# Feed-forward up projections of a hybrid encoder trunk by a seven-product block algorithm, with one arena of buffers and smaller down groups

## The chip, the cores and the metric

The kernel runs on one core of a Trainium2 chip. The metric is the device time of one execution in microseconds (us), the median of several runs. The matrix engine is PE (TensorE), its weight loads are shown apart as PEld; DVE is VectorE, ACT is ScalarE, POOL is GpSimd, SP is SyncE, whose queue issues the weight loads from device memory.

## The reference

Two batches of tokens, one of 512 and one of 256, go through a trunk of two layers with shared weights. The width is 1024, the inner width of a feed-forward network (FFN) is 2816. Cut to what matters:

```python
def rmsnorm(x, g):
    return x * rsqrt(mean(x * x, axis=-1) + 1e-6) * g

def swiglu_ffn(x, w1, w2):
    gate, up = split(x @ w1, 2, axis=-1)       # w1: 1024 x 5632
    return (silu(gate) * up) @ w2              # w2: 2816 x 1024

# a layer; mixer: layer 0 bidirectional HGRN2, layer 1 windowed attention
x = x + 0.5 * swiglu_ffn(rmsnorm(x, g0), w1a, w2a)
x = x + mixer(rmsnorm(x, g1))
x = x + 0.5 * swiglu_ffn(rmsnorm(x, g2), w1b, w2b)
# after the last layer: y = rmsnorm(x, g)
```

All data are fp32. There are four FFNs: the first, then the HGRN2 mixer, then the second and the third one behind the other, then the attention mixer, then the fourth.

## The kernel before

**Layout.** Activations lie transposed: 1024 features are eight tiles of 128 partitions (index m or k, constant `NC`), tokens are columns. The two batches are `s = 0` with 512 columns and `s = 1` with 256 (`SEQS`); the residual is `self.x[s][m]`.

**Precision.** An fp32 operand is split into a high part (rounded to fp32r) and a low part (the rest). A product of two split operands is three matmuls into one PSUM bank: high·high, high·low, low·high (`mm3`, L175–179). Operands are split by a copy on ACT and a subtraction on DVE: `split` (L181–183) for activations, and `stage_next` (L139–153) for weights, with the cast at L148 and the subtraction at L149. The subtraction is on DVE or, for the first two columns of an FFN (`early`), on POOL.

**Weights.** `plan_ffn` puts all weight tiles of an FFN in a list in the order of their use. `load_next` issues the load of the next one on SP into a raw tile (`wr`, two buffers), and `stage_next` splits it into `wh` and `wl` (`WBUFS` = 4 of each). When the last matmul that reads a tile has been issued, `done` frees it and stages the next (`ahead`). So the staging instructions stand in ACT's and DVE's order at the place where a tile came free, between the operations of the column that is being computed, and each engine works through its instructions in that order.

**FFN.** The 22 columns of the inner width (128 each; a column has a gate tile and an up tile of weights) are taken in groups, `FFN_GROUPS = (7, 7, 6, 2)`. For each column `ffn_up` (L358–378) computes, for both batches in turn, gate and up by 8 k-blocks × 3 matmuls each, then Silu on ACT (L375), the product on DVE (L376), and the split of the hidden tile. After the columns of a group `ffn_down` (L380) multiplies the hidden tiles of the group by their rows of `w2` for each of the eight output tiles, and `add_x` (L388–393) adds half of the result to the residual. In the last group, of two columns, batch 0 is finished first (up, then down), then batch 1, so that the norm of batch 0 can run beside batch 1's matmuls.

**Norm.** `after_x` squares each finished residual tile and sums the squares (`sumsq`, L249–261: POOL or DVE at L259). `norm_steps` (L281–311) is a list of steps for a batch: the statistics (`rstd`, L265–279, small matmuls at L273), and two `apply` steps of four tiles each, with the normalisation on DVE (L304), the high part on ACT (L306) and the low part on DVE and POOL in turn (L308), into the operands `self.h[s][m]`. `later` puts steps on a list and `run_later` takes the next one; the calls stand between the matmuls of the next stage, so they set where the norm stands in each engine's order. For the first FFN, `enter` in `load_x` (L203–229) makes the operands from the loaded tokens.

**Memory.** `big` tiles (12 of them) hold hidden tiles, mixer data and other large things; the normed operands have a pool of their own (`hp`).

Names in rows: ps is a PSUM bank, h a normed operand, wr a raw weight tile, wh and wl its parts, tA and tB temporaries (512 and 256 columns), big a large tile, x the residual.

Of the kernel before, what the change touches and what calls it, by code (L numbers as in the profile page):

```python
# [13 lines left out]
ALU = mybir.AluOpType  # L14
# [20 lines left out]
FFN_GROUPS = (7, 7, 6, 2)  # L35
WBUFS = 4


class Trunk:
    def __init__(self, ctx, tc, consts):  # L40
# [4 lines left out]
        self.hp = pool("hp")  # L45
# [19 lines left out]
    def tmp(self, n, dt=F32):  # L65
        tag, bufs, size = ("tA", 7, TA) if n > TB else ("tB", 4, TB)
        t = self.tp.tile([P, size], dt, tag=tag, name=self.name(tag), bufs=bufs)
        return t[:, :n]

    def big(self, shape, dt=F32):  # L70
        return self.ap.tile(shape, dt, tag="big", name=self.name("big"), bufs=12)
# [9 lines left out]
    def ht(self, s, part):  # L81
        n = (TA, TB)[s]
        return self.hp.tile([P, n], F32R, tag=f"h{s}{part}", name=self.name("h"), bufs=8)
# [27 lines left out]
    def load_tables(self):  # L111
# [3 lines left out]
        mf = self.wp.tile([P, LEVELS + 1, P], F32, tag="wr", name="mf", bufs=2)  # L115
# [10 lines left out]
    def plan(self, key, src, shape, eng, spare=False):  # L126
        self.queue.append((key, src, shape, eng, spare))

    def load_next(self):
        key, src, shape, eng, spare = self.queue.pop(0)  # L130
        raw = self.wtile("wr", F32, 2, shape)
        self.last_load = self.nc.sync.dma_start(raw, src.rearrange("(k p) c -> p k c", p=P))
        self.loaded.append((key, raw, shape, eng, spare))

    def wtile(self, tag, dt, bufs, shape):
        t = self.wp.tile([P, 1024], dt, tag=tag, name=self.name(tag), bufs=bufs)
        return t[:, : shape[0] * shape[1]].rearrange("p (a b) -> p a b", a=shape[0])

    def stage_next(self):  # L139
        if not self.loaded:  # L140
            self.load_next()
        key, raw, shape, eng, spare = self.loaded.pop(0)
        if spare:
            n = shape[0] * shape[1]
            hi, lo = (self.big([P, 1024], F32R)[:, :n].rearrange("p (a b) -> p a b", a=shape[0]) for _ in range(2))
        else:
            hi, lo = (self.wtile(tag, F32R, WBUFS, shape) for tag in ("wh", "wl"))
        self.nc.scalar.copy(hi, raw)  # L148
        eng.tensor_sub(lo, raw, hi.bitcast(F32))  # L149
        self.staged[key] = (hi, lo, spare)  # L150
        self.held += not spare
        while self.queue and len(self.loaded) < 2:
            self.load_next()
# [6 lines left out]
    def done(self, key):  # L160
        self.held -= not self.staged.pop(key)[2]
        self.ahead()

    def ahead(self):
        while (self.queue or self.loaded) and self.held < WBUFS:
            self.stage_next()
# [18 lines left out]
    def load_x(self, srcs):  # L185
# [17 lines left out]
        def enter(s):  # L203
# [19 lines left out]
            self.h[s] = []  # L223
            for m in range(NC):
                g = self.cols[:, m : m + 1]
                hi, lo = self.ht(s, "h"), self.ht(s, "l")
                order[-1] = nc.scalar.activation(hi, pt(m), AF.Copy, scale=g).ins
                nc.vector.scalar_tensor_tensor(lo, pt(m), g, hi.bitcast(F32), ALU.mult, ALU.subtract)
                self.h[s].append((hi, lo))
# [17 lines left out]
        self.later(lambda: enter(1), lambda: None, lambda: None, lambda: None, residual)  # L247
# [33 lines left out]
    def norm_steps(self, s, row):  # L281
# [14 lines left out]

        def apply(part):
# [3 lines left out]
            for m in range(4 * part, 4 * part + 4):  # L301
                g = self.cols[:, row * NC + m : row * NC + m + 1]
                t = self.tmp(n)
                nc.vector.scalar_tensor_tensor(t, self.x[s][m], g, box["pb"], ALU.mult, ALU.mult)  # L304
                hi, lo = self.h[s][m]
                nc.scalar.copy(hi, t)  # L306
                eng = nc.gpsimd if m % 2 else nc.vector
                eng.tensor_sub(lo, t, hi.bitcast(F32))  # L308

        self.h[s] = [(self.ht(s, "h"), self.ht(s, "l")) for _ in range(NC)]  # L310
        return stats, lambda: apply(0), lambda: apply(1)
# [27 lines left out]
    def plan_ffn(self, tag, w1, w2):  # L339
        early, late = self.nc.gpsimd, self.nc.vector  # L340

        def up(j, spare=False):
            for c in (j, NF + j):
                eng = early if j < 2 else late
                self.plan((tag, "up", c), w1[:, c * P : (c + 1) * P], (NC, P), eng, spare)

        j = 0
        for gi, n in enumerate(FFN_GROUPS):
            last = gi == len(FFN_GROUPS) - 1
            for i in range(n):  # L350
                up(j + i, last and i == 0)
            width = 4 * P if last else P
            for c in range(D // width):
                src = w2[j * P : (j + n) * P, c * width : (c + 1) * width]
                self.plan((tag, "down", gi, c), src, (n, width), late)
            j += n

    def ffn_up(self, tag, j, seqs, hid):  # L358
        nc = self.nc
        keys = [(tag, "up", c) for c in (j, NF + j)]  # L360
        for s in seqs:
            off, n = SEQS[s]
            pss = []
            for key in keys:
                wh, wl = self.take(key)
                ps = self.ps(n)
                for k in range(NC):
                    self.mm3(ps, (wh[:, k, :], wl[:, k, :]), self.h[s][k], k == 0, k == NC - 1)
                    if k in ((6,), (4, 6))[key == keys[1]] if s == 0 else (k == NC - 1 and key == keys[0]):
                        self.run_later()  # L370
                if s:
                    self.done(key)
                pss.append(ps)
            a, u = self.tmp(n), self.tmp(n)
            self.last_act = nc.scalar.activation(a, pss[0], AF.Silu).ins  # L375
            self.last_dve = nc.vector.tensor_mul(u, a, pss[1]).ins  # L376
            self.split(u, hid[:, 0, off : off + n], hid[:, 1, off : off + n])
            self.run_later()
# [16 lines left out]
    def ffn(self, tag, next_row):  # L395
        j = 0
        for gi, n in enumerate(FFN_GROUPS[:-1]):
            hids = [self.big([P, 2, T], F32R) for _ in range(n)]
            for i in range(n):
                self.ffn_up(tag, j + i, (0, 1), hids[i])  # L400
            j += n
            for m in range(NC):
                key = (tag, "down", gi, m)
                w = self.take(key)
                for s in range(2):
                    self.ffn_down(s, m, hids, *w)
                self.done(key)
        hids = [self.big([P, 2, T], F32R) for _ in range(FFN_GROUPS[-1])]
        for s in range(2):
            for i, hid in enumerate(hids):  # L410
                self.ffn_up(tag, j + i, (s,), hid)
            for m in range(NC):
                key = (tag, "down", gi + 1, m // 4)
                c = (m % 4) * P
                self.ffn_down(s, m, hids, *(t[:, :, c : c + P] for t in self.take(key)))
                if s and m % 4 == 3:
                    self.done(key)
                self.after_x(s, m, next_row)
                if s and m < NC - 1:
                    self.run_later()  # L420
# [356 lines left out]
    def swa(self, next_row):  # L777
# [48 lines left out]
        out = [[None] * NC, [None] * NC]  # L826
        of = {}
# [371 lines left out]
```

## Time and profile before

| | |
|---|---|
| time, median of 3 runs | 3131.28 us (3129.14 to 3134.45) |
| span of the profiled execution (its own time) | 3127.9 us |
| instructions in the span | 42175 |
| PE busy | 3071.7 us, 17765 matmuls |
| PEld busy | 2705.4 us |
| DVE busy | 1313.4 us, 2254 instructions |
| ACT busy | 931.3 us, 1677 instructions |
| POOL busy | 407.5 us, 294 instructions |
| moved by DMA | 199.18 MB, mean 64 GB/s |

The profile is that of one execution. A busy time is the sum of the times of an engine's instructions; the matmuls of PE overlap in their records (one starts before the end of the one ahead is recorded), so that the cost of a matmul in a full stream is the distance between two starts. An instruction's row names its line, the operation, output and inputs with their sizes, and, in brackets, how long its engine was idle before it and what ended that. The granted clock is the share of full speed at which PE was allowed to run.

### The profile page before, as it was taken

The page shows a single profiled execution, that of the slowest core. Times are in us where ns is not written, and L with a number is a line of the kernel's source. Part 1 is how long each engine was busy: PE and PEld are TensorE (multiplying, and loading weights), DVE is VectorE, ACT ScalarE, POOL GpSimd, SP SyncE. Part 2 cuts the span into 40 slices and gives each one's busy share as a digit, 9 for nine tenths or more (in the row PEclk, how much of TensorE's full clock was granted, in tenths as well). Part 3 has the DMA queues.
Part 4 walks back from the last instruction along what each step waited for, and adds up shares of the span by engine and source line. Part 5 has one row for each costly group of instructions (what it writes and reads, how often), then busy time and mean ns, then how long its engine had stood idle before and what let it go on. Part 6 is the DMA issues. An engine that isn't in the chain of part 4 may idle for free.

```text
span 3127.9 us, 42175 instructions
## 1 busy us (share of the span) xinstructions
PE 3071.7 (98%) x17765; PEld 2705.4 (86%) x17765; DVE 1313.4 (42%) x2254; ACT 931.3 (30%) x1677; POOL 407.5 (13%) x294
## 2 busy tenths in 40 slices
PE   8999999999999999999999999999999999999998
PEld 7888888888898888888888888888877878888887
DVE  4222223467477562322234322222459862323233
ACT  4212121433333432121223311212357752121122
POOL 1000000354443130000002000000113440000000
PEclk9999999999999999999999999999999999999999
DMA  3222222211110322222221222221222112222221
GB/s 120 65 64 65 65 61 75 80 56 41 41 41 28 108 68 66 67 64 61 68 63 52 61 65 64 61 68 54 82 72 63 41 44 64 70 61 61 68 72 57
DMA packets 324797, 199.18 MB, mean 64 GB/s; under 512 B 7208, under 2 KB 308736, under 8 KB 324608
## 3 DMA queue, kind: packets, MB, share of 16 engines
q1 hardware_dynamic: 314688, 183.07, 19.6%
q10 hardware_dynamic: 9920, 13.43, 1.3%
q8 instruction: 139, 2.28, 0.3%
q14 instruction: 50, 0.41, 0.0%
HBM read 187.03 MB, written 9.44 MB: 63 GB/s over the span
## 4 chain that ended last, share of the span: by engine, by line
PE 92%; DVE 4%; ACT 2%; issue 1%; POOL 1%; DMA 1%; POOLq 0%; DVEq 0%; SPq 0%; ACTq 0%
PE ps L178 28%; PE ps L177 28%; PE ps L179 28%; PE ps L531 3%; PE ps L626 1%; PE ps L602 1%; DMA wr<-in_ffn_w_dram 0%; PE ps L1061 0%; ACT wh L148 0%; POOL tA L259 0%; DVE h L308 0%; DVE tB L259 0%; PE ps L273 0%; ACT big L1038 0%; PE ps L1022 0%
## 5 line engine op out<-in xcount | busy, mean ns | idle before, releaser
L177 PE MATMUL ps<-h,wh 128*128 128x256 f32 (+1 forms) x3200 | 1087.6, 340 | 0.1
L178 PE MATMUL ps<-h,wh 128*128 128x256 f32 (+1 forms) x3200 | 1080.1, 338 | 3.3 <-POOL h L308 3.1
L179 PE MATMUL ps<-h,wl 128*128 128x256 f32 (+1 forms) x3200 | 1077.8, 337 | 0.0
L178 PEld LDWEIGHTS ps<-h,wh 128*128 128x128 f32 x3200 | 609.4, 190 | 67.1 <-POOL h L308 4.6
L177 PEld LDWEIGHTS ps<-h,wh 128*128 128x128 f32 x3200 | 609.6, 191 | 64.2 <-issue 1.0
L179 PEld LDWEIGHTS ps<-h,wl 128*128 128x128 f32 x3200 | 608.7, 190 | 64.0
L148 ACT CAST wh<-wr 128x1024 fp32r<-128x1024 f32 (+2 forms) x344 | 346.7, 1008 | 848.7 <-PE ps L178 686.9
L177 PE MATMUL ps<-big,wh 128*128 128x256 f32 (+1 forms) x1536 | 519.0, 340 | 6.9 <-DVE tA L304 6.1
L178 PE MATMUL ps<-big,wh 128*128 128x256 f32 (+1 forms) x1536 | 520.2, 339 | 2.8 <-DVE big L183 2.8
L179 PE MATMUL ps<-big,wl 128*128 128x256 f32 (+1 forms) x1536 | 518.5, 338 | 0.1
L149 DVE TENSOR_TENSOR wl<-wr,wh 128x1024 fp32r<-128x1024 f32 (+2 forms) x276 | 322.0, 1167 | 220.7 <-ACT wh L148 218.5
L376 DVE TENSOR_TENSOR tA<-tA,ps 128x512 f32<-128x512 f32 x88 | 60.5, 687 | 717.7 <-PE ps L179 717.7
L177 PEld LDWEIGHTS ps<-big,wh 128*128 128x128 f32 x1536 | 292.7, 191 | 40.6 <-DVE tA L304 6.7
L259 POOL TENSOR_TENSOR tA<-tA,tA 128x512 f32<-128x512 f32 x36 | 46.5, 1293 | 2138.6 <-ACT tA L257 2137.0
L178 PEld LDWEIGHTS ps<-big,wh 128*128 128x128 f32 x1536 | 294.5, 192 | 34.6 <-DVE big L183 4.4
L179 PEld LDWEIGHTS ps<-big,wl 128*128 128x128 f32 x1536 | 294.4, 192 | 31.1 <-DVE wl L149 0.3
L393 DVE SCALAR_TENSOR_TENSOR x<-ps,x 128x256 f32<-128x256 f32 (+1 forms) x256 | 141.9, 557 | 398.7 <-PE ps L179 398.4
L182 ACT CAST big<-tA 128x512 fp32r<-128x512 f32 x88 | 54.5, 619 | 476.0 <-DVE tA L376 476.0
L149 POOL TENSOR_TENSOR wl<-wr,wh 128x1024 fp32r<-128x1024 f32 x68 | 166.3, 2450 | 148.7 <-ACT wh L148 145.3
L375 ACT ACTIVATE tA<-ps 128x512 f32<-128x512 f32 x88 | 52.6, 598 | 357.4 <-PE ps L179 357.4
L177 PE MATMUL ps<-wh,h 128*128 128x512 f32 x336 | 135.0, 402 | 0.6 <-DVE stat L1025 0.6
L578 DVE TENSOR_TENSOR big<-big,big 128x384 f32<-128x384 f32 x168 | 127.8, 806 | 15.5 <-ACT big L556 13.8
(183 smaller groups left out, 2784.9 us busy)
## 6 DMA issues: line engine op xcount, KB each, us to landing
wr<-in_ffn_w_dram SPq DMA_DIRECT2D x184, 512.0 KB, 3.8
wr<-in_ffn_w_dram SPq DMA_DIRECT2D x64, 448.0 KB, 3.3
wr<-in_hg_w_in_dram SPq DMA_DIRECT2D x40, 512.0 KB, 3.7
wr<-in_ffn_w_dram SPq DMA_DIRECT2D x32, 384.0 KB, 3.1
wr<-in_hg_w_o_dram SPq DMA_DIRECT2D x12, 512.0 KB, 3.6
wr<-in_sw_w_qkv_dram SPq DMA_DIRECT2D x12, 512.0 KB, 3.5
spill<-x ACTq DMA_DIRECT2D x16, 256.0 KB, 2.0
x<-spill ACTq DMA_DIRECT2D x16, 256.0 KB, 2.8
```

The source lines that it names most:

```text
L148: self.nc.scalar.copy(hi, raw)
L149: eng.tensor_sub(lo, raw, hi.bitcast(F32))
L177: nc.tensor.matmul(out, a[0], b[0], start=first, stop=False)
L178: nc.tensor.matmul(out, a[0], b[1], start=False, stop=False)
L179: nc.tensor.matmul(out, a[1], b[0], start=False, stop=last)
L182: self.nc.scalar.copy(hi, src)
L259: (nc.vector if s or m == NC - 1 else nc.gpsimd).tensor_add(self.acc[s], self.acc[s], t)
L375: self.last_act = nc.scalar.activation(a, pss[0], AF.Silu).ins
L376: self.last_dve = nc.vector.tensor_mul(u, a, pss[1]).ins
L393: self.nc.vector.scalar_tensor_tensor(x, ps, c, x, ALU.mult, ALU.add)
L531: nc.tensor.matmul(pss[s][:, i * P : (i + 1) * P], lhs(b), rhs(b), start=True, stop=True)
L578: eng.tensor_mul(xv, xv, t[td][1 - par])
```

## The change

**Seven products.** The first group of an FFN, now two columns, is computed as before (`up_plain`), except that the 768 tokens are taken as two halves of 384 columns instead of 512 and 256. Each of the other 20 columns is computed by `up_pair`: gate and up tile are seen as a 2×2 matrix of blocks (rows: gate and up; columns: features 0–511 and 512–1023), and the activations as another (features 0–511 and 512–1023; token halves 0 and 1). The product of two such matrices is made from seven block products instead of eight, in Winograd's form: seven times 4 k-blocks × 3 matmuls of 384 columns.

- The activations' sums `t1` to `t4` are made once per FFN by `sum_steps`: 16 sums on POOL, each then split on ACT and DVE. The blocks `b00`, `b10`, `b01` and `b11` are split by `put_half`. The step list of the norm is longer by these four steps.
- The weights' sums are made on DVE in `pair_steps`, which replaces the staging of a tile by seven steps, one for each product (`p1`, `p6`, `p2`, `p7`, `p5`, `p4`, `p3`): four sums of 512 elements, and for each product a cast on ACT and a subtraction, on DVE but for `p5`, whose is on POOL.
- The products' results are joined in `up_pair`: where two products are only added, they are accumulated in one PSUM bank; the rest is one copy on ACT and five additions or subtractions on DVE, between the products. Two banks are used twice: product `p2` is added to the bank that ACT has just copied, `p4` and `p3` to banks that DVE has just read.

**Groups.** `FFN_GROUPS = (2, 4, 4, 4, 4, 4)`: down projections come after two, then after every four columns. In the last group all columns' ups come first, then the down projection of batch 0, then that of batch 1. The last group's down weights are loaded and split twice, once for each batch.

**Buffers.** `hp` is gone; `SLOTS` = 18 big tiles hold the operands, sums and hidden tiles. Staged weights share `WBUFS` = 8 tiles of one kind (high and low part of a pair's product lie in one), raw weights have `RAWBUFS` = 4, `tA` has 9 buffers. The mixers' operands (`self.h`) are in big tiles too.

The diff, cut to its core:

```diff
-FFN_GROUPS = (7, 7, 6, 2)
-WBUFS = 4
+FFN_GROUPS = (2, 4, 4, 4, 4, 4)
+H = T // 2
+WBUFS = 8
+RAWBUFS = 4
+SLOTS = 18
...
+    def pair_steps(self, key, one, two):
...
+        a11, a12, a21, a22 = flat(one, 0), flat(one, 1), flat(two, 0), flat(two, 1)
...
+        def split(name, src, eng):
+            w = self.wtile()
+            hi, lo = w[:, :512], w[:, 512:]
+            nc.scalar.copy(hi, src)
+            eng.tensor_sub(lo, src, hi.bitcast(F32))
...
+        def p6():
+            box["s3"] = self.tmp(512)
+            nc.vector.tensor_add(box["s3"], a11, a21)
+            nc.vector.tensor_add(a21, a21, a22)
+            nc.vector.tensor_add(a11, a11, a21)
+            split("p6", a11, nc.vector)
...
+    def sum_steps(self):
...
+        def go(k):
+            b11, b12, b21, b22 = (self.block(i // 2, i % 2, k) for i in range(4))
+            t = {n: self.tmp(H) for n in ("t1", "t3", "t2", "t4")}
+            nc.gpsimd.tensor_sub(t["t1"], b11, b12)
+            nc.gpsimd.tensor_sub(t["t3"], b12, b22)
+            nc.gpsimd.tensor_add(t["t2"], t["t1"], b22)
+            nc.gpsimd.tensor_sub(t["t4"], b21, t["t2"])
+            for n, src in t.items():
+                self.split(src, *self.operand(n, k))
...
+    def up_pair(self, tag, j, hid):
...
+        self.product(key, "p1", "b00", a, True, False)
+        nc.scalar.copy(v, a)
+        self.product(key, "p6", "t2", b, True, True)
+        nc.vector.tensor_sub(v, v, b)
+        self.product(key, "p2", "b10", a, False, True)
+        nc.scalar.activation(g, a, AF.Silu)
+        self.product(key, "p7", "t3", c, True, False)
+        nc.vector.tensor_sub(w, c, v)
+        self.product(key, "p5", "t1", d, True, False)
+        nc.vector.tensor_sub(w, w, d)
+        self.product(key, "p4", "t4", c, False, True)
+        nc.vector.tensor_sub(u, c, v)
+        nc.vector.tensor_mul(u, u, g)
+        self.split(u, hid[:, 0, :H], hid[:, 1, :H])
+        self.product(key, "p3", "b11", d, False, True)
+        nc.vector.tensor_add(v, v, d)
+        self.last_act = nc.scalar.activation(v, v, AF.Silu).ins
+        self.last_dve = nc.vector.tensor_mul(v, v, w).ins
+        self.split(v, hid[:, 0, H:], hid[:, 1, H:])
...
+            if gi == 0:
+                for half in range(2):
+                    for i in range(n):
+                        self.up_plain(tag, i, half, hids[i])
+                self.run_later(len(self.deferred))
+            else:
+                for i in range(n):
+                    self.up_pair(tag, j + i, hids[i])
...
+            for s in range(2):
+                for m in range(NC):
+                    down(s, m, s, True)
+                    self.after_x(s, m, next_row)
+                    if s and m < NC - 1:
+                        self.run_later(1 if next_row is not None else 2)
```

In the new code the lines of the steps named later are: cast and subtraction of a product's weights L167 and L168 (of a plain tile, L152 and L153), the weights' sums L177, L178, L179 and L183, the split of an activation L239 (ACT) and L240 (DVE), the sums on POOL L411–414, the plain columns' product of gate and up L486, the matmul of a product L494, the joining operations L510 (ACT), L512, L516, L518, L520, L521, L524 and L526 (DVE), the addition to the residual L542.

PE's order in one column of the third FFN, before: with each of its two weight tiles 24 matmuls of 512 columns, of which the first two k-blocks with the up tile are shown (wh and wl are the parts of that tile, h those of the normed operand); the same follows for 256 columns.

```order
L177 MATMUL ps_13815<-h_13193,wh_13654 128x512
L178 MATMUL ps_13815<-h_13194,wh_13654 128x512
L179 MATMUL ps_13815<-h_13193,wl_13655 128x512
L177 MATMUL ps_13815<-h_13195,wh_13654 128x512
L178 MATMUL ps_13815<-h_13196,wh_13654 128x512
L179 MATMUL ps_13815<-h_13195,wl_13655 128x512
```

After, a whole column is 14 such rows of six matmuls: seven products, each with one tile w and two big tiles of the operand (here the first pair of the third FFN).

```order
L494 MATMUL ps_14651<-big_13997,w_14456 128x384 x6
L494 MATMUL ps_14651<-big_14002,w_14456 128x384 x6
L494 MATMUL ps_14652<-big_14264,w_14463 128x384 x6
L494 MATMUL ps_14652<-big_14325,w_14463 128x384 x6
L494 MATMUL ps_14651<-big_14028,w_14491 128x384 x6
L494 MATMUL ps_14651<-big_14033,w_14491 128x384 x6
L494 MATMUL ps_14653<-big_14261,w_14494 128x384 x6
L494 MATMUL ps_14653<-big_14322,w_14494 128x384 x6
L494 MATMUL ps_14654<-big_14258,w_14566 128x384 x6
L494 MATMUL ps_14654<-big_14319,w_14566 128x384 x6
```

The bank 14651 is written by the first product and, with the second one between them, again by the third; the second product's operand 14264 is one of the sums `t2`.

DVE's order at the start of the third FFN, before: behind the normalisation of batch 1 (L304, L308) come at once the first column's product (L376), its split (L183) and the staging of weights (L149).

```order
L304 SCALAR_TENSOR_TENSOR tB_13585<-x_8573,cols,ps_13549 128x256
L308 TENSOR_TENSOR h_13488<-tB_13581,h_13487 128x256
L376 TENSOR_TENSOR tA_13593<-tA_13592,ps_13533 128x512
L183 TENSOR_TENSOR big_13491<-tA_13593,big_13491 128x512
L149 TENSOR_TENSOR wl_13624<-wr_13421,wh_13623 128x1024
L376 TENSOR_TENSOR tB_13661<-tB_13660,ps_13629 128x256
L149 TENSOR_TENSOR wl_13655<-wr_13471,wh_13654 128x1024
```

After, behind the normalisation stand 16 splits of sums (L240, the last four of them shown), and only then the first plain column's product (L486) and the staging of the first pair's weights (L177, L168).

```order
L240 TENSOR_TENSOR big_14319<-tA_14343,big_14319 128x384
L240 TENSOR_TENSOR big_14322<-tA_14344,big_14322 128x384
L240 TENSOR_TENSOR big_14325<-tA_14345,big_14325 128x384
L240 TENSOR_TENSOR big_14328<-tA_14346,big_14328 128x384
L486 TENSOR_TENSOR tA_14359<-tA_14359,ps_14298 128x384
L153 TENSOR_TENSOR w_14390<-wr_13982,w_14389 128x1024
L240 TENSOR_TENSOR big_14141<-tA_14359,big_14141 128x384
L153 TENSOR_TENSOR w_14419<-wr_14056,w_14418 128x1024
L486 TENSOR_TENSOR tA_14426<-tA_14426,ps_14393 128x384
L177 TENSOR_TENSOR tA_14459<-wr_14134,wr_14136 128x512
L168 TENSOR_TENSOR w_14456<-wr_14134,w_14456 128x512
```

So the first pair's first weights (14456) stand in DVE's order behind all splits of the sums and behind the first plain column's results.

DVE's order in a pair in the middle of a group: joining operations (L512 to L526, each bound to a product that PE has just finished) and staging for the next pair (L168, L177 to L183) in turn.

```order
L512 TENSOR_TENSOR tA_14791<-tA_14791,ps_14788 128x384
L168 TENSOR_TENSOR w_14811<-wr_14640,w_14811 128x512
L168 TENSOR_TENSOR w_14827<-wr_14640,w_14827 128x512
L183 TENSOR_TENSOR wr_14640<-wr_14640 128x512
L168 TENSOR_TENSOR w_14843<-tA_14807,w_14843 128x512
L516 TENSOR_TENSOR tA_14792<-ps_14789,tA_14791 128x384
L518 TENSOR_TENSOR tA_14792<-tA_14792,ps_14790 128x384
L168 TENSOR_TENSOR w_14875<-wr_14642,w_14875 128x512
L520 TENSOR_TENSOR tA_14794<-ps_14789,tA_14791 128x384
L177 TENSOR_TENSOR tA_14943<-wr_14759,wr_14761 128x512
```

Before, these were for a column four rows of results (L376, L183 for each batch) and two of staging (L149).

More of the change, by code (lines that the diff above doesn't have):

```diff
@@ L141, in stage_next @@
             self.load_next()
[L142 to L152, printed above, removed]
+        steps = self.loaded[0][1]
+        n, go = steps.pop(0)
+        go()
+        self.held += n
+        if not steps:
+            self.loaded.pop(0)
+        while self.queue and sum(e[0] for e in self.loaded) + len(self.queue[0][1]) <= RAWBUFS:
             self.load_next()
@@ L358, in ffn_up @@
-    def ffn_up(self, tag, j, seqs, hid):
-        nc = self.nc
[L360 to L378, printed above, removed]
+            for i in range(j, j + n):
+                gate, up = (w1[:, c * P : (c + 1) * P] for c in (i, NF + i))
+                if gi:
+                    self.plan_pair((tag, i), gate, up)
+                else:
+                    self.plan((tag, i, 0), gate, (NC, P), early)
+                    self.plan((tag, i, 1), up, (NC, P), early)
@@ new lines, in plan_ffn, with gated @@
+            width = P * max(1, 8 // n)
+            for turn in range(2 if gi == len(FFN_GROUPS) - 1 else 1):
+                for c in range(D // width):
+                    src = w2[j * P : (j + n) * P, c * width : (c + 1) * width]
+                    self.plan((tag, "down", gi, turn, c), src, (n, width), late)
+            j += n
+    def gated(self, gate, up, hid, half):
+        hi, lo = (hid[:, i, half * H : (half + 1) * H] for i in range(2))
+        self.last_act = self.nc.scalar.activation(gate, gate, AF.Silu).ins
+        self.last_dve = self.nc.vector.tensor_mul(gate, gate, up).ins
+        self.split(gate, hi, lo)
@@ new lines, in product @@
+    def product(self, key, name, src, ps, first, last):
+        wh, wl = self.take((*key, name))
+        for k in range(4):
+            a, b = (wh[:, k, :], wl[:, k, :]), self.operand(src, k)
+            for i, (x, y) in enumerate(((0, 0), (0, 1), (1, 0))):
+                self.nc.tensor.matmul(
+                    ps,
+                    a[x],
+                    b[y],
+                    start=first and k == 0 and i == 0,
+                    stop=k == 3 and i == 2,
+                    skip_group_check=True,
+                )
+        self.done((*key, name))
```

195 lines of the change are left out of this document (134 added, 61 removed).

## The prediction

> **What bounds the kernel now.** I read the page first: busy time by engine, the chain that ended last, and the tenths of the granted clock.
>
> ```profile
> span 3127.9 us, 42175 instructions
> PE 3071.7 (98%) x17765; PEld 2705.4 (86%) x17765; DVE 1313.4 (42%) x2254; ACT 931.3 (30%) x1677; POOL 407.5 (13%) x294
> PE 92%; DVE 4%; ACT 2%; issue 1%; POOL 1%; DMA 1%; POOLq 0%; DVEq 0%; SPq 0%; ACTq 0%
> ```
>
> PE is busy 98% of the span and carries 92% of the chain; the rest is short stops. Next come the windows: one long stretch of the second FFN, the seam into the third, and the starts of the second and fourth. The columns are length, then busy time (and count) of PE, PEld, DVE, ACT, POOL, then granted clock, DMA share and GB/s.
>
> ```profile
> 1160.00:1705.00 545.00, 544.90 (x3122) 481.19 (x3121) 169.10 (x232) 121.44 (x179) 16.58 (x14) 1.00 0.21 61
> 1705.00:1730.00 25.00, 20.52 (x99) 17.38 (x97) 17.27 (x29) 13.06 (x23) 11.55 (x7) 0.86 0.29 85
> 1151.00:1160.00 9.00, 4.12 (x15) 3.30 (x15) 5.89 (x4) 3.62 (x8) 6.14 (x3) 0.82 0.42 119
> 2555.00:2560.00 5.00, 1.89 (x8) 1.20 (x7) 5.00 (x8) 3.32 (x7) 5.00 (x3) 0.96 0.35 105
> ```
>
> Inside an FFN, PE stands still for 0.1 us in 545, at full clock, while DVE works 31% of the time and ACT 22%. So the inside of an FFN costs what its matmuls cost. At the seams PE both stops and, afterwards, runs at a lower clock: in 1705–1730 4.5 us are idle and 14% of 25 us, 3.5 us, go in clock, 8.0 in all. At 1151 it is 4.9 idle and 1.6 in clock, 6.5; at 2555 it is 3.3.
>
> The price of a matmul is the distance between starts, since the records overlap. The next rows are the first and last of a run of 27 matmuls of 512 columns, of 48 of 256, and four neighbours of 384 in the attention, all with 128x128 weights.
>
> ```profile
> 99.86 0.39 PE L177 MATMUL ps<-h,wh 128*128 128x512 f32 x1
> ...
> 105.76 0.39 PE L179 MATMUL ps<-h,wl 128*128 128x512 f32 x1
> 105.98 0.28 PE L177 MATMUL ps<-h,wh 128*128 128x256 f32 x1
> 106.10 0.19 PEld L179 LDWEIGHTS ps<-h,wl 128*128 128x128 f32 x1
> ...
> 111.62 0.28 PE L179 MATMUL ps<-h,wl 128*128 128x256 f32 x1
> 2338.32 0.33 PE L1022 MATMUL ps<-big,tA 128*128 128x384 f32 x1
> ...
> 2338.84 0.35 PE L1023 MATMUL ps<-big,tA 128*128 128x384 f32 x1
> ```
>
> That is 5.90/26 = 0.227 us for 512 columns, 5.64/47 = 0.120 for 256 and 0.52/3 = 0.173 for 384; halfway between the first two lies 0.1735. I take 0.174.
>
> **The change, part by part. 1. Matmuls.** Before, the up projections of one FFN are 44 weight tiles × 8 k-blocks × 3 products = 1056 matmuls at each width: 1056 × (0.227 + 0.120) = 366.4 us. After, two of 22 columns stay plain (4 tiles × 8 × 3 × 2 halves = 192 matmuls of 384), and 20 pairs take 7 products × 4 k-blocks × 3 = 84 each: 1872 × 0.174 = 325.7. The saving is 40.7 per FFN, 163 us for four. The down projections keep their 1056 per FFN and width. A pair takes 84 × 0.174 = 14.6 us where it took 16.7, and a product 2.09.
>
> The Trainium skill ("TensorE: Matmul & The Clock Gate", section "Wait — 56ns, not 53.3ns?") puts the warm start-to-start at N/2.4 GHz plus some 2.5 ns. By it the four FFNs would save 4 × (1056 × 0.325 − 1872 × 0.1625) = 156 us, an estimate; the rows above lie about 11 ns higher per matmul, and they decide.
>
> **2. Does the cover hold inside a pair?** Prices of the operations by shape:
>
> ```profile
> L183 DVE TENSOR_TENSOR big<-tA,big 128x512 fp32r<-128x512 f32 x88 | 60.9, 692 | 59.7 <-ACT big L182 59.7
> L376 DVE TENSOR_TENSOR tA<-tA,ps 128x512 f32<-128x512 f32 x88 | 60.5, 687 | 717.7 <-PE ps L179 717.7
> L376 DVE TENSOR_TENSOR tB<-tB,ps 128x256 f32<-128x256 f32 x88 | 37.0, 421 | 73.5 <-PE ps L179 73.5
> L182 ACT CAST big<-tA 128x512 fp32r<-128x512 f32 x88 | 54.5, 619 | 476.0 <-DVE tA L376 476.0
> L182 ACT CAST big<-tB 128x256 fp32r<-128x256 f32 x94 | 38.0, 404 | 12.5 <-DVE tB L376 11.7 <-DVE tB L772 0.8
> L259 POOL TENSOR_TENSOR tA<-tA,tA 128x512 f32<-128x512 f32 x36 | 46.5, 1293 | 2138.6 <-ACT tA L257 2137.0
> L308 POOL TENSOR_TENSOR h<-tB,h 128x256 fp32r<-128x256 f32 x20 | 15.5, 776 | 59.9 <-ACT h L306 59.9
> L149 DVE TENSOR_TENSOR wl<-wr,wh 128x1024 fp32r<-128x1024 f32 x180 | 221.5, 1231 | 153.8 <-ACT wh L148 151.6 <-ACT tB L375 2.2
> ```
>
> At 384 columns I take the mean of 512 and 256: DVE 0.55, ACT 0.51, POOL 1.03. A pair puts on DVE ten operations of 512 (six weight splits L168, sums L177, L178, L179, L183) and nine of 384 (L512 to L526, two splits L240): 10 × 0.69 + 9 × 0.55 = 11.9 us, 81% of 14.6. ACT has 7 × 0.62 + 5 × 0.51 = 6.9; POOL one split of 1.29. PE waits for others at three places: p2 reuses the bank that ACT copies at L510, p4 the bank read at L516, p3 the one read at L518. Each has one product, 2.09 us, between, and one read of about 0.55 in it; the slack of 1.5 us is the cover, and weights are staged up to eight products ahead. I cost the inside of a pair at nothing; if the cover is gone, each 0.5 us per pair is 40 us over 80 pairs.
>
> **3. Start of an FFN.** This term costs time. Before, plain up projections of 512 + 256 columns follow the norm and cover 7 columns × 16.7 us of work. After, the plain part is 192 × 0.174 = 33.4 us, and by its end the operand sums t1 to t4 must be there. Seam rows:
>
> ```profile
> 1702.13 2.48 DVE L308 TENSOR_TENSOR h<-tA,h 128x512 fp32r<-128x512 f32 x1
> 1704.02 1.74 POOL L308 TENSOR_TENSOR h<-tA,h 128x512 fp32r<-128x512 f32 x1
> 1707.68 0.38 PE L177 MATMUL ps<-big,wh 128*128 128x256 f32 x1 [2.03 <-DVE tA L304]
> 1156.55 1.75 PE L273 MATMUL ps<-ones,tB 128*128 128x1 f32 x8 [4.88 <-DVE tB L259]
> L308 DVE TENSOR_TENSOR h<-tA,h 128x512 fp32r<-128x512 f32 x20 | 24.8, 1240 | 0.2
> L308 POOL TENSOR_TENSOR h<-tA,h 128x512 fp32r<-128x512 f32 x20 | 30.8, 1546 | 41.4 <-ACT h L306 41.4
> L304 DVE SCALAR_TENSOR_TENSOR tA<-x,cols,ps 128x512 f32<-128x512 f32 x40 | 28.3, 738 | 1.2 <-PE ps L300 1.2
> L304 DVE SCALAR_TENSOR_TENSOR tB<-x,cols,ps 128x256 f32<-128x256 f32 x40 | 17.3, 473 | 15.7 <-PE ps L300 15.7
> L393 DVE SCALAR_TENSOR_TENSOR x<-ps,x 128x256 f32<-128x256 f32 x128 | 53.8, 422 | 154.0 <-PE ps L179 154.0
> ```
>
> After the last down matmul of the short sequence DVE has, in its order: the statistics, about 6 us (the 4.88 idle and the matmuls after it); eight L304 of 0.473 and eight splits of 0.55 with the diagonal, 9.3; the 16 splits of the sums, each behind a POOL sum of 1.03; then 5.5 us of rows (two L486, two L153, a split, L177, L168) until the first weights of the first pair are there. Without interference the POOL sums set the third step: 16.5, in all 37.3 against 33.4 of PE, 4 us late. But L308, DVE and POOL side by side, takes 1.24 on DVE where L183 takes 0.69, and 1.55 on POOL where L259 takes 1.29. With POOL's 1.2 the third step is 19.8 and PE waits 7, and the next rows (L178, L179, L168 for the second and third products) catch up with another 2 to 4: I take 10. If the two engines alternate strictly (1.03 + 0.55 per sum, 25 us) it is 14 to 17. Such a stop costs a further 3.4 in clock, as in 1705–1730: 13 per FFN.
>
> The Trainium skill ("SBUF — State Buffer", section "Who interferes with whom") says that a DVE operation with two SBUF inputs and a GpSimd operation that reads SBUF exclude each other for a whole operation. L308 at nearly twice the time of L183 agrees; applied in full it gives 14 rather than 10 per FFN, 16 us more in the sum, about 3050.
>
> Net of what stops there before: first FFN +13; second 13 − 6.5 = +6.5; fourth 13 − 3.3 = +10. The third follows an FFN, and its long sequence must be normalised while PE runs the short sequence's last stage: before 96 up matmuls and 48 down ones of 256 (17.3 us), after only 96 down ones (11.5). DVE has eight L304 (5.9), eight splits (4.4), eight L393 (3.4), seven sums of squares (2.9) and some six weight tiles with the diagonal (8) in it, about 25. Some 13 late there and 13 at the sums, minus the 8.0 of before, is +18; I take +20. Together +50.
>
> **4. The mixers' starts** after the first and third FFN lose the same 6 us of cover, though fewer fresh buffers are waited for: I take half, 3 each, +6 (bounds 0 and 12).
>
> **5. Up to down.** The last pair of a group ends with L524, Silu, product, cast and split: 0.55 + 0.51 + 0.55 + 0.51 + 0.55 = 2.7 plus up to 2 us of queue, against the first down matmuls on other columns (9 + 9 of 0.227, 4.1). I take 0.5 for each of 20 groups, +10 (bounds 0 and 20).
>
> Sum: −163 + 50 + 6 + 10 = −97 on the profiled span of 3127.9, 3031. The median of the runs shown, 3131.28, lies 3.4 above that span, so 3034.
>
> **Rivals.** B, the starts are covered: if POOL's sums run ahead while PE is in the plain part, only the handovers remain, some 23 us: 3127.9 − 163 + 23 + 3.4 = 2991. For it speaks the first window: 0.1 us idle in 545. Against it the count of 37 us against 33.
>
> C, DVE a little over in the pairs: 81% is an average, its order is fixed, and a product read late holds up weight staging behind it. At 15.2 us per pair, 0.6 more, 80 pairs give +48, so 3082; at 15.6 it is 3114.
>
> D, slower: DVE becomes the bound of the pairs. 11.9 us, plus a blocked 1.3 beside POOL's split, plus 19 short waits of 0.22 each in a chain of PE, ACT and DVE:
>
> ```profile
> 1714.72 0.42 DVE L393 SCALAR_TENSOR_TENSOR x<-ps,x 128x256 f32<-128x256 f32 x1 [0.22 <-PE ps L179]
> ```
>
> That makes 17.4 per pair, 2.8 × 80 = 224 over the forecast, 3258. It decides from 14.6 + 97/80 = 15.8 us per pair on. Against it: the waits fall only where DVE runs out of ready work, and staging fills such holes.
>
> E, weight loads bind: one load takes 0.19 by the PEld row. Then 1872 × 0.19 = 355.7, only 11 per FFN saved, 43, and 3127.9 − 43 + 66 + 3.4 = 3154, slower. Against it: the 256-wide matmuls start every 0.120 with the same loads.
>
> F, the change doesn't do what it says: the built order shows 84 matmuls per pair and 16185 in all; no chance kept.
>
> **How the numbers follow.** A, the forecast, 0.60; B 0.23; C 0.11; D 0.04; E 0.02. A's own range is 3005 to 3065: starts between 4 and 17 each and the bounds of parts 4 and 5. The whole range runs from B less part of its handovers, 2975, into C, 3090; above it lie D, E and some of C. About 0.2%, 6 us, is what a measurement of this kernel can tell from no change. Faster by more: A, B and nearly all of C, 0.93; within it 0.02; slower 0.05.
>
> **What would show it.** Right: steady pairs of 14.6 us with PE without gaps; PE waiting on DVE before the first pair of each FFN, about 10 us, followed by a low granted clock; POOL sums slowed beside DVE splits; DVE near 1.95 ms busy (1313 + 80 × 7.2, and some 60 for the sums and the smaller down groups; 7.2 is 11.9 less the 4.7 that a column cost before, by the rows L149, L376 and L183). Wrong: pairs beyond 15.2 us with DVE above 95% in them (C, D); no gap at the first pair (B); 384-wide matmuls starting every 0.19 (E); or a long wait at the third FFN's first matmuls above 20 us, which would put the seam, not the sums, first.

## The result and the profile after

The changed kernel takes 3045.51 us (median of runs from 3040.99 to 3045.94) against 3130.21 us of the kernel before on the same chip: a ratio of 0.9727, 95% interval 0.9713 to 0.9741. The forecast was 3034 us with a range of 2975 to 3090. The profiled execution spans 3043.3 us, so the sum of the forecast, −97 us on the span of 3127.9, has −84.6 to compare with.

The head of the page of the changed kernel: span, then busy time, share and instructions of each engine.

```profile
span 3043.3 us, 42529 instructions
PE 2935.9 (96%) x16805; PEld 2722.8 (89%) x16805; DVE 2013.2 (66%) x3510; ACT 1175.8 (39%) x2233; POOL 570.2 (19%) x414
```

DVE has 700 us more to do, near the 1.95 ms that were forecast, and PE is busy for a smaller share than before: it has less work and stands still more. First the inside of the FFNs: the matmuls of the products as a group (in the last field the idle time of PE ahead of them), and a window over the four pairs of one group of the second FFN, with the columns as in the prediction.

```profile
L494 PE MATMUL ps<-big,w 128*128 128x384 f32 x6720 | 1171.1, 334 | 0.0
1291.10:1349.50 58.40, 58.40 (x338) 58.21 (x338) 40.61 (x67) 25.34 (x44) 3.88 (x3) 1.00 0.30 88
```

Not one of the 6720 product matmuls follows a stop of PE, and the four pairs take 58.4 us, 14.6 each, as forecast. DVE is busy for 40.6 us of them, 70% where 81% was counted. Then the waits of PE, longest in total first (total us, times, longest one):

```profile
PE ps L234 <- ACT big L239: 30.9, 7, 8.2
PE ps L330 <- DVE tB L316: 8.8, 3, 4.4
...
PE ps L235 <- DVE w L153: 6.4, 3, 3.8
...
PE ps L235 <- DVE big L240: 4.1, 4, 3.2
```

L234 is the first matmul of a plain or down triple, L239 the cast that splits an activation: PE waits seven times, for up to 8.2 us, for a split operand: once in the first FFN and twice at the start of each of the others. The place is seen at the start of the second FFN: PE's rows that wait, then DVE's, then POOL's (start, length, and in brackets the idle time and what ended it).

```profile
1174.08 0.80 PE L234 MATMUL ps<-big,w 128*128 128x512 f32 x1 [3.42 <-ACT big L239]
1181.59 1.01 PE L234 MATMUL ps<-big,w 128*128 128x512 f32 x2 [3.74 <-ACT big L239]
```

```profile
1150.54 0.55 DVE L486 TENSOR_TENSOR tA<-tA,ps 128x384 f32<-128x384 f32 x1
1151.67 18.68 DVE L240 TENSOR_TENSOR big<-tA,big 128x384 fp32r<-128x384 f32 x17 [0.58 <-ACT big L239]
1170.27 0.54 DVE L486 TENSOR_TENSOR tA<-tA,ps 128x384 f32<-128x384 f32 x1
...
1172.94 0.54 DVE L486 TENSOR_TENSOR tA<-tA,ps 128x384 f32<-128x384 f32 x1
...
1178.51 0.69 DVE L177 TENSOR_TENSOR tA<-wr,wr 128x512 f32<-128x512 f32 x1 [1.50 <-DMA wr<-in_ffn_w_dram]
1179.24 0.69 DVE L178 TENSOR_TENSOR wr<-wr 128x512 f32<-128x512 f32 x1
1179.85 0.68 DVE L168 TENSOR_TENSOR w<-wr,w 128x512 fp32r<-128x512 f32 x1
1180.45 0.55 DVE L486 TENSOR_TENSOR tA<-tA,ps 128x384 f32<-128x384 f32 x1
```

```profile
1162.85 1.33 POOL L411 TENSOR_TENSOR tA<-big 128x384 f32<-128x384 f32 x1
1164.15 1.32 POOL L412 TENSOR_TENSOR tA<-big 128x384 f32<-128x384 f32 x1
```

DVE finishes one plain result (L486) at 1150.5, then splits for 18.7 us (17 splits, 16 of them of sums) at POOL's pace of 1.3 us per sum, and only at 1170.3 turns to the next result. PE has been through the plain matmuls by then and waits at the first down matmul (128x512, 1174.08), which reads both halves of the first column and so needs the result at 1172.94 as well. The second stop, at 1181.59, is the last result's: its L486 at 1180.45 stands on DVE behind staging that waited 1.5 us for a load. So the stops lie in the down stage of the first group, not at the first pair. In the first FFN they stand elsewhere: 3.94 us at the first plain matmul, and 2.83 and 2.67 us at transposes of the tokens for the residual (L294), which wait for DVE and ACT.

To add this up I take from the trace the distance of each pair of neighbouring matmul starts, less the full-stream price (0.227, 0.1735 or 0.120 us by width); what is over half a price is a stop or a low clock. (Narrower matmuls, as many before as after, have a price each too.) The work left at these prices is 2937.6 us before and 2771.1 after. The excess by place, in one profiled execution of each kernel:

| place | before | after | e5 (below) |
|---|---|---|---|
| first 100 us (first FFN) | 15.3 | 33.2 | 23.5 |
| into the HGRN2 mixer | 7.9 | 15.0 | 10.3 |
| start of the second FFN | 10.5 | 19.6 | 7.8 |
| start of the third FFN | 10.4 | 26.5 | 15.5 |
| into the attention mixer | 7.2 | 13.6 | 11.7 |
| start of the fourth FFN | 10.8 | 27.4 | 9.9 |
| everything else | 103.0 | 111.3 | 110.3 |

A place can differ by some 5 us without any other stop. The stretch into the HGRN2 mixer of the changed kernel, and of e7 (below), which leaves that stage as it is:

```profile
520.00:585.00 65.00, 58.52 (x284) 49.80 (x283) 41.82 (x69) 29.41 (x53) 20.75 (x14) 0.89 0.41 130
520.00:585.00 65.00, 58.55 (x303) 49.68 (x302) 44.03 (x74) 31.01 (x58) 22.86 (x16) 0.97 0.41 130
```

PE stands still for the same 6.5 us in both, but the clock is 0.89 in one and 0.97 in the other.

### The profile page after: what moved, and what is told of

Read it like the earlier page. It is cut to its first block, busy times and chain, and to the rows that moved or that the text cites. A ratio compares the mean times of both kernels' runs of the same rounds, so it can differ in the third digit from the quotient of the medians.

```text
span 3043.3 us, 42529 instructions
## 1 busy us (share of the span) xinstructions
PE 2935.9 (96%) x16805; PEld 2722.8 (89%) x16805; DVE 2013.2 (66%) x3510; ACT 1175.8 (39%) x2233; POOL 570.2 (19%) x414
## 5 line engine op out<-in xcount | busy, mean ns | idle before, releaser
L494 PE MATMUL ps<-big,w 128*128 128x384 f32 x6720 | 1171.1, 334 | 0.0
L494 PEld LDWEIGHTS ps<-big,w 128*128 128x128 f32 x6720 | 1163.4, 188 | 3.7 <-DVE tA L518 3.7
L234 PE MATMUL ps<-big,w 128*128 128x256 f32 (+2 forms) x2304 | 793.8, 347 | 30.9 <-ACT big L239 30.9
L235 PE MATMUL ps<-big,w 128*128 128x256 f32 (+2 forms) x2304 | 789.4, 343 | 6.8 <-DVE big L240 4.1
L236 PE MATMUL ps<-big,w 128*128 128x256 f32 (+2 forms) x2304 | 784.6, 341 | 0.0
L167 ACT CAST w<-wr 128x512 fp32r<-128x512 f32 x480 | 290.1, 621 | 834.1 <-issue 330.4
L234 PEld LDWEIGHTS ps<-big,w 128*128 128x128 f32 x2304 | 444.7, 193 | 78.9 <-ACT big L239 35.3
L235 PEld LDWEIGHTS ps<-big,w 128*128 128x128 f32 x2304 | 445.8, 193 | 51.5 <-DVE big L240 6.5
L236 PEld LDWEIGHTS ps<-big,w 128*128 128x128 f32 x2304 | 444.7, 193 | 42.0
L168 POOL TENSOR_TENSOR w<-wr,w 128x512 fp32r<-128x512 f32 x80 | 102.9, 1286 | 1656.2 <-ACT w L167 1656.2
L542 DVE SCALAR_TENSOR_TENSOR x<-ps,x 128x512 f32<-128x512 f32 (+1 forms) x384 | 210.7, 556 | 251.9 <-PE ps L236 250.8
L168 DVE TENSOR_TENSOR w<-wr,w 128x512 fp32r<-128x512 f32 x400 | 284.7, 725 | 69.7 <-ACT w L167 61.6
L152 ACT CAST w<-wr 128x1024 fp32r<-128x1024 f32 x192 | 201.3, 1050 | 227.9 <-PE ps L235 96.0
L153 DVE TENSOR_TENSOR w<-wr,w 128x1024 fp32r<-128x1024 f32 x124 | 151.4, 1223 | 74.4 <-PE ps L494 65.4
L153 POOL TENSOR_TENSOR w<-wr,w 128x1024 fp32r<-128x1024 f32 x68 | 167.2, 2468 | 177.0 <-ACT w L152 175.7
L240 DVE TENSOR_TENSOR big<-tA,big 128x384 fp32r<-128x384 f32 x240 | 160.7, 685 | 22.3 <-ACT big L239 22.1
L239 ACT CAST big<-tA 128x384 fp32r<-128x384 f32 x240 | 121.2, 513 | 104.8 <-DVE tA L521 33.5
L235 PE MATMUL ps<-w,big 128*128 128x512 f32 x336 | 134.3, 400 | 6.4 <-DVE w L153 6.4
L234 PE MATMUL ps<-w,big 128*128 128x512 f32 x336 | 137.6, 410 | 0.0
L236 PE MATMUL ps<-w,big 128*128 128x512 f32 x336 | 134.0, 399 | 0.0
L518 DVE TENSOR_TENSOR tA<-tA,ps 128x384 f32<-128x384 f32 x80 | 44.2, 553 | 91.4 <-PE ps L494 91.4
```

Source lines behind the costliest of these rows:

```text
L167: nc.scalar.copy(hi, src)
L168: eng.tensor_sub(lo, src, hi.bitcast(F32))
L234: nc.tensor.matmul(out, a[0], b[0], start=first, stop=False)
L235: nc.tensor.matmul(out, a[0], b[1], start=False, stop=False)
L236: nc.tensor.matmul(out, a[1], b[0], start=False, stop=last)
L239: self.nc.scalar.copy(hi, src)
```

## The experiments

The theory at this point: the pairs give all their matmuls; what is lost is lost at the six seams, most of it by the sums' place in DVE's order. The rivals: POOL and DVE shutting each other out wherever the sums stand; the shorter cover for the norm; and DVE close under PE in the pairs.

**e1: the sums behind the results.** The four steps leave the list of the norm; two come behind the first half's plain columns, two into the down loop.

```diff
-        return (*steps, *self.sum_steps()) if s and feeds_ffn else steps
+        return steps
...
+                    if half == 0:
+                        self.run_later(len(self.deferred))
+                        sums.pop(0)()
+                        sums.pop(0)()
...
+                    if gi == 0 and m % 2 == 0 and sums:
+                        sums.pop(0)()
```

> The steps of the operand sums are moved: two behind the first half's plain results, two into the down projection of the first group. Theory (the sums stand in DVE's and ACT's order ahead of the plain columns' results, and the first down matmuls wait for those): the first stop of 4 to 8 us goes at the starts of the second, third and fourth FFN, with its low clock, so 20 to 28 us less, 3018 to 3026. Rival (POOL and DVE shut each other out for the same 20 us wherever the sums stand, so that the wait only moves to the first pair): 3040 to 3050.

Measured: 3019.41 us, ratio to before 0.9646 (0.963 to 0.9662). The 26 us are those of the theory. One stop, of 4.1 us, is left at the second FFN's start.

**e2: weight tiles given back behind the results.** In `up_plain` the two calls of `done` move behind the split.

> As the run before, and the plain columns' weight tiles are given back only behind their results, so that the staging of the first pairs, which waits for a load, no longer stands ahead of the last plain results on DVE. Theory: the second stop of 2 to 4 us goes too, with its clock, 10 to 15 us less than the run before, 3005 to 3012. Rival (the load is late anyway, and the first pair now waits for its weights): the same as the run before or some us more.

Measured: 3014.52 us, 0.9627 (0.9613 to 0.9641), 5 us less instead of 10 to 15, and with intervals that overlap those of e1. DVE's rows at the second FFN's start tell why; the last L484 is the last plain result (L486 of the changed kernel):

```profile
1164.88 0.68 DVE L179 TENSOR_TENSOR wr<-wr,wr 128x512 f32<-128x512 f32 x1
1165.48 2.29 DVE L240 TENSOR_TENSOR big<-tA,big 128x384 fp32r<-128x384 f32 x3
1167.70 0.54 DVE L484 TENSOR_TENSOR tA<-tA,ps 128x384 f32<-128x384 f32 x1
```

The scheduler that sets DVE's order from the code still puts weights' sums and three splits of sums ahead of it. Moving code didn't move the instructions far enough.

**e5: the results held first.** As e2, with that order forced:

```diff
+            with self.tc.issue_after(self.plain_last) if j else nullcontext():
+                for c in range(2):
+                    self.done((tag, j, c))
...
+                        with self.tc.issue_after(self.plain_last):
+                            sums.pop(0)()
```

> As e2, and the staging of the first pairs' weights and the last two steps of sums may only be issued behind the split of the last plain column, so that nothing stands ahead of it on DVE. Theory: the stop of 3 to 5 us that e2 still has at the first down matmul goes at three starts, with its low clock, 10 to 18 us less than e2, 2997 to 3005. Rival (the sums then come too late for the second product of the first pair, or the first weights do): 3010 to 3020, with the stop at the first pair.

Measured: 2990.18 us, 0.9557 (0.9542 to 0.9573), 55 us less than the changed kernel with the same work on every engine. At the starts of the second, third and fourth FFN the waits for split operands are gone; of the 30.9 us one wait is left, in the first FFN:

```profile
PE ps L234 <- ACT big L239: 3.9, 1, 3.9
```

The same stretch of changed kernel (75 us) and e5 (80 us):

```profile
1125.00:1200.00 75.00, 63.17 (x337) 58.83 (x337) 59.81 (x88) 27.42 (x54) 32.60 (x21) 0.86 0.20 57
```

```profile
1110.00:1190.00 80.00, 75.60 (x438) 72.88 (x437) 66.37 (x106) 33.81 (x67) 34.91 (x22) 0.96 0.23 67
```

PE goes from 63 of 75 to 76 of 80 and its clock from 0.86 to 0.96, while POOL still makes all its sums.

**e3: no sums at all**, `sum_steps` empty and the products reading `b` blocks instead.

> The 16 sums per FFN and their splits are left out, and the products read other blocks in place of the sums, so that the operands are not those of the algorithm. Theory (the sums are the main price of the starts): 30 to 40 us less than the changed kernel, 3005 to 3015. Rival (the starts are late because the norm has less cover behind the last down projection, and by the longer way from the norm to the split operands): under 12 us less, 3033 or more.

Measured: 2987.69 us, 0.9546 (0.9532 to 0.956). The sums cost 58 us in the changed kernel, 14.5 per FFN: more than expected here, and near the 13 per start of the forecast. e5, with all the sums, is only 2.5 us slower, which is within the intervals of the two runs: nearly all of the cost was order.

**e8: sums on DVE**, four times `nc.vector` for `nc.gpsimd` in `sum_steps`, nothing else.

> The changed kernel with the 16 sums on DVE instead of POOL, order otherwise as it is. Theory (the stop is the length of the row of sums in DVE's order, 20.6 us with POOL, 17.6 without): 3 us less at each of three or four starts, 3033 to 3040. Rival (mutual blocking of POOL and DVE is the price of the sums): 3015 or less.

Measured: 3009.11 us, 0.9615 (0.96 to 0.9629), 36 us less; the number is that of the rival. One sum and a split on DVE:

```profile
1157.68 0.55 DVE L240 TENSOR_TENSOR big<-tA,big 128x384 fp32r<-128x384 f32 x1
1158.15 0.55 DVE L414 TENSOR_TENSOR tA<-big,tA 128x384 f32<-128x384 f32 x1
1158.61 1.49 DVE L240 TENSOR_TENSOR big<-tA,big 128x384 fp32r<-128x384 f32 x3
```

They start every 0.47 us, 0.94 for sum and split against 1.3 beside POOL, and the row of sums takes 15.6 us (1148.2 to 1163.8) where it took 18.7. But the built order changed elsewhere too: the last plain result now stands ahead of the staging that waits for a load. Two edits in one, then, and the next run takes one of them alone.

**e10: only the staging held back**; the sums stay on POOL and in their place.

> The changed kernel with one edit: the staging of what follows the plain columns may only be issued behind the last plain column's split; the sums stay where they were, on POOL. Theory (the second stop of 2 to 4 us at the starts is the wait of DVE for a load, in a staging step that stands ahead of the last plain result): that stop and its low clock go, 3028 to 3035. Rival (only the sums are late, and the gain of e8 was the blocking between POOL and DVE alone): 3040 to 3047.

Measured: 3025.43 us, 0.9664 (0.9648 to 0.968), 20 us less: the second stop is worth more than I had given it. At the second FFN's start one stop of over 1 us is left, the first (L485 is the cast of a plain result here):

```profile
1169.51 0.79 PE L234 MATMUL ps<-big,w 128*128 128x512 f32 x1 [2.80 <-ACT big L485]
```

The other 16 us of e8 would then be the shorter row of sums: by the count of starts e8 lies below e10 by 5, 4 and 7 us at the second, third and fourth FFN, and by 1 at the first. No run has the shorter row alone.

**e6: e5 with the sums on DVE.**

> As e5, with the 16 sums on DVE instead of POOL. Theory (POOL and DVE each stretch the other, 1.3 and 1.1 us per sum, while DVE alone does sum and split in 2 x 0.55): the sums take 17.6 us instead of 20.6 and are no longer on the path, so within 5 us of e5. Rival (the mutual blocking is what makes the starts late): 15 us or more less than e5.

Measured: 3008.41 us, 0.9612 (0.9598 to 0.9626), 18 us more than e5. Neither expectation. PE's waits in the first down stage of the second FFN show a new one:

```profile
1175.32 0.50 PE L234 MATMUL ps<-big,w 128*128 128x512 f32 x1 [1.23 <-DVE x L545]
1181.39 0.50 PE L234 MATMUL ps<-big,w 128*128 128x512 f32 x1 [1.59 <-DVE x L545]
```

L545 adds a down result to the residual and so frees its bank; it now stands behind sums and splits on DVE. There are eight such waits, 11.3 us in all. With the order of e5, the sums on POOL cost next to nothing (e3) and those on DVE do: leaving POOL is of use only where the row of sums stands ahead of what PE needs next.

**e9: the first FFN's operands straight from PSUM**, on top of e5: for the first 384 tokens ACT writes the high part and DVE the low part from the transposed tokens.

> As e5, and for the first 384 tokens of the first FFN the split operands are made straight from PSUM, high part on ACT and low part on DVE, with the copies that the sums need behind them. Theory (the first FFN's start loses some 8 us against the kernel before since ACT makes a copy and then a cast of it ahead of the first matmul): 4 to 8 us less than e5, 2982 to 2986. Rival (the start waits for loads and for the transposes of the tokens): as e5, 2988 to 2993.

Measured: 2989.35 us, 0.9546 (0.9532 to 0.956), the same as e5. PE waits 3.7 us for its first split operand where it waits 3.9 in e5. So the copy ahead of the split isn't what holds the kernel's start; what does stays open.

**e11: a longer last stage.** As e5, the last group's down matmuls of the short batch made twice.

```diff
+        hids = hids * times
...
-        self.add_x(s, m, ps, 0.5)
+        self.add_x(s, m, ps, 0.5 / times)
```

> As e5, and in the last group the down matmuls of the short batch are made twice and added with half the factor: 4 x 11.5 = 46 us more of PE, as cover for the norm of the long batch. Theory (the norm of the long batch is late because its cover shrank from 17.3 to 11.5 us, some 4 us at each of four seams): 46 less some 12 to 18, so 3018 to 3024. Rival (these stops hang on chains that the cover does not touch): 3033 to 3038.

Measured: 3005.48 us, 0.9599 (0.9585 to 0.9614): 46 us of added matmuls cost 15. Around the start of the third FFN, e5 first, then e11:

```profile
1598.00:1700.00 102.00, 95.87 (x509) 87.30 (x509) 76.34 (x116) 47.03 (x82) 40.12 (x27) 0.92 0.21 63
```

```profile
1598.00:1700.00 102.00, 102.00 (x616) 95.10 (x616) 74.21 (x115) 45.21 (x81) 40.70 (x27) 1.00 0.23 68
```

With 23 us of cover instead of 11.5 PE doesn't stop at all here and its clock stays at 1.00. By the count of starts the seams into both mixers and the third FFN fall from 10.3, 11.7 and 15.5 us to 1.9, 1.9 and 2.1. The cover is nearly all of what is left there; before, with 17.3, the same three cost 7.9, 7.2 and 10.4.

**e7 and e12: DVE's reserve in the pairs.** The changed kernel, writing each pair's six low parts on DVE twice (e7) or three times (e12).

```diff
-            eng.tensor_sub(lo, src, hi.bitcast(F32))
+            for _ in range(2 if eng is nc.vector else 1):
+                eng.tensor_sub(lo, src, hi.bitcast(F32))
```

> In every pair the six low parts of the weights that DVE makes are written twice, 6 x 0.69 = 4.1 us more DVE work per pair and no other change. Theory (DVE has slack in the pairs: 40.6 of 58.4 us in one group's pairs): DVE goes to some 57 of 58.4 us, and the time rises by less than 20 us, 3045 to 3065. Rival (a chain of waits of DVE lies just under PE, 17.4 us per pair were feared): the pairs grow by 1.5 us or more, 3165 or more.

> In every pair the six low parts of the weights that DVE makes are written three times, 8.3 us more DVE work per pair. Theory (DVE has a limit that e7 had not reached): one group's pairs then ask 40.6 + 33 = 74 of DVE in 58.4 us, of which some can move into the down stage; the time rises by between 56 us (pairs and down stage together, 94.6 of 91.8 us per group) and 300 us: 3100 to 3350. Rival (DVE is nowhere near a bound): 3045 to 3060.

Measured: e7 3043.31 us, 0.9724 (0.9709 to 0.9738); e12 3227.82 us, 1.031 (1.0295 to 1.0325). A group's pairs in e7, then in e12, without the last 24 of the 336 product matmuls, which stand behind some down matmuls in e12's built order:

```profile
1289.00:1347.00 58.00, 58.00 (x334) 57.71 (x333) 50.87 (x86) 24.79 (x43) 6.15 (x3) 1.00 0.30 91
```

```profile
1246.10:1307.60 61.50, 57.11 (x314) 55.33 (x313) 55.83 (x96) 21.05 (x40) 9.18 (x3) 0.97 0.18 55
```

At 50.9 of 58 us, 88%, DVE costs PE nothing; with another 4.1 us per pair PE stops with DVE at 91%, the pairs take 16.4 to 16.9 us and all of the gain is lost. The longest of PE's stops in the pairs is for POOL's split of `p5` (L169 here), which runs beside a row of six subtractions on DVE:

```profile
1294.51 13.28 PE L495 MATMUL ps<-big,w 128*128 128x384 f32 x66 [3.37 <-POOL w L169]
1290.54 3.92 POOL L169 TENSOR_TENSOR w<-wr,w 128x512 fp32r<-128x512 f32 x1 [14.14 <-ACT w L167]
1289.04 3.69 DVE L169 TENSOR_TENSOR w<-wr,w 128x512 fp32r<-128x512 f32 x6
```

There are 20 such stops, one per group, 67.6 us in all. The split on POOL takes 1.29 us on average in the changed kernel, 1.84 in e7 and 2.74 in e12. So more work on DVE met its bound partly through POOL; no run parts the two. The bound lies between e7 and e12, and it is met under 100%, as rival D said, but 4 us or more per pair from where the kernel stands.

**e4: no pairs.** All columns plain, the rest of the change kept, no sums.

> All 22 columns plain, in halves of 384; arena, groups, staging tiles and the last group's order as in the changed kernel; no sums. Theory (the seven products give exactly their matmuls, 166 us, and the rest of the change costs its seams): 40.7 us per FFN come back, and without the sums some 35 are saved, so 3045 + 163 - 35 = 3173, or down to 3150 if the seams lose less without pairs. Rival (arena and small groups cost nothing, the whole loss hangs on the pairs and sums): 3131, the time of before.

Measured: 3159.99 us, 1.0094 (1.0079 to 1.0109). Against e3, which differs by the pairs alone, the seven products are worth 172 us (166 by count of matmuls); the groups, halves, arena and the last group's order cost 29 against the kernel before.

## Why the prediction was right

**1. Matmuls: right.** −163 was forecast, −166.5 is counted; the difference is the price of 0.174 for 0.1735. The trace has 16805 matmuls, 960 fewer than before, as four FFNs with 1056 × 2 − 1872 less must have; the 16185 named with rival F is not its number.

**2. Inside the pairs: right.** Nothing was charged, nothing is lost, with 14.60 us per pair in all 20 groups. Rivals C and D fall by the same rows, and by e7 with 4.1 us of reserve. E falls too: the loads' records average 0.19, but the matmuls start every 0.174 on average.

**3. Starts: nearly right in size, wrong in place.** +50 was forecast; the four starts cost 17.9, 9.1, 16.1 and 16.6 more than before, +59.7, of which e5 takes away 50.0 by order alone. The step that failed is that the sums and "the first weights of the first pair" are needed when the plain part ends: the down stage of the first group, 16.7 us of PE, stands ahead of the first pair, and I had left it out. With it, my count of 40.6 us of steps stands against 50.1 of PE and gives no stop, which was rival B; and no gap at the first pair, the sign that I had named for B, is what the trace shows. That 13 per start came near the measured cost is luck. The sums had time enough, and what was late at the second, third and fourth FFN was the plain columns' results, which stood behind the sums in DVE's order and which that down stage needs. The difference matters: a late sum would have needed less work or another engine; a late result needed another order, as e5 shows. In the first FFN the stops are others, and 8.2 of its 17.9 us stay in e5 with the cause open. The pace taken for the sums, 19.8 us for 16, was right: the row took 18.7, and 16 at 1.29 make 20.6. The 3.4 for the clock is 3.5 by the window that it was taken from. By the rule of the Trainium skill ("SBUF — State Buffer", section "Who interferes with whom") taken in full, a sum and a split would follow each other; here they take 1.3 us where they take 1.02 and 0.47 apart, so they overlap a little, and the stretch of both agrees.

**4. Mixers' starts:** +6 forecast, +13.5 measured. e11 shows that more cover takes these stops away. How much of the 13.5 is cover is less sure: with the cover as it is, e5 has 6.6 of it less, and up to 5 of that is the clock behind the same stops into the HGRN2 mixer. The forecast put the size at half.

**5. Up to down:** +10 forecast, 0 measured. The last results of a group were in time at every handover.

The rest, +8 us outside the six seams, a good part of it in the attention mixer, was not in the sum and wasn't tested; its cause stays open. So −166.5 + 59.7 + 13.5 + 8.3 = −85.0, against −84.6 of the span: starts, mixers and the rest came out 9.7, 7.5 and 8.3 dearer than forecast, matmuls and handovers 3.5 and 10 cheaper, which makes the 12 us between the two sums: the errors cancel in part. Rival B, 2991 with the starts covered, is what e5 measures (2990.18), by the way that the rival named: the sums do run ahead beside the plain part and the down stage, once nothing waits behind them. That the number is so near is partly chance: B's 23 us were to be lost at handovers, and up to down lost nothing.

## What to carry to other kernels

When work leaves the bounding engine, look at what the helper engines have to do at the seams, where PE has only one short stage to run: the inside of the loop had room, the seams had none. On an engine that works in order, side work that is needed late costs nothing only if it stands behind the result that is needed next; look for the place in the built order, since moving code alone (e2) didn't do it. Count every stage that lies between a producer and its consumer before calling it late, and test a suspected lack of cover by adding work that does nothing: 46 us of matmuls that cost 15 say more than a sum of waits.

## What the runs showed of the hardware

- POOL and DVE side by side stretch each other. In the changed kernel, a POOL sum beside DVE operations that read PSUM (second FFN), and a DVE split beside POOL's sums (fourth FFN):

```profile
1144.21 1.02 POOL L411 TENSOR_TENSOR tA<-big 128x384 f32<-128x384 f32 x1 [9.02 <-DVE big L363]
```

```profile
2523.10 1.13 DVE L240 TENSOR_TENSOR big<-tA,big 128x384 fp32r<-128x384 f32 x1 [0.16 <-ACT big L239]
```

  Beside splits a sum takes 1.33, and a split alone 0.55; a sum and a split come every 1.29 us. On DVE alone, operations recorded at 0.55 start every 0.47 (e8). Beside a longer row on DVE, POOL is held longer: 3.92 us in e12 for a split that takes 1.29 on average in the changed kernel.
- A stop costs PE again in clock: in the changed kernel the granted clock is 0.86 over 75 us with 12 us of stops, in e11 1.00 over 102 us with none. The cost isn't fixed: with the same 6.5 us of stops in 65 the clock was 0.89 in one kernel and 0.97 in another.
- PE was held up in e12's pairs with DVE at 91% busy, not at 100%; at 88% in e7 it wasn't. The longest stops in e12 were for POOL's split beside DVE's row, so the share of DVE's busy time alone doesn't say where the bound lies.
